# The order of an attention step on three engines, evictions one tick later, and three PSUM banks for the scores

## The chip, the cores and the metric

The kernel runs on one core of a Trainium2 chip. A core has a matrix engine (PE), a vector engine (DVE), an activation engine (ACT), a general engine (POOL) and a queue engine (SP), each with an instruction queue of its own that is worked off strictly in order. PE writes to eight PSUM banks, and DVE and ACT read them; everything else lies in SBUF. The metric is the device time of one launch in microseconds (us), the median over several runs.

## The reference

One layer of an encoder with two kinds of attention heads, run on a prompt of 1024 tokens and a sample of 512 tokens with the same weights; d_model is 1024, a head is 64 wide.

```python
hn = rms_norm(x, g_attn)
qa, ka, va, qd, kd, vd = split(hn @ w_in, 6)
oa = neighbourhood_attention(qa, ka, va, rpb)   # 8 heads, 8 x 16 window on a grid 64 wide
od = dilated_attention(qd, kd, vd, slopes)      # 8 heads, (window, dilation) = (128,1),(512,4),(2048,16)
x = x + concat(rms_norm(oa, g_na), rms_norm(od, g_dil)) @ w_out
x = x + (silu(rms_norm(x) @ w_gate) * (rms_norm(x) @ w_up)) @ w_down
y = rms_norm(x, g_final)
```

Each attention block is a softmax: `s = q k^T + bias`, `p = exp(s - max)`, `o = p v / sum(p)`. The whole is in float32.

## The kernel before

**Pairs and blocks.** The heads go in pairs: 16 pairs, first eight of the prompt, then eight of the sample, dilated ("b") and neighbourhood ("a") in turn: prompt b 0, prompt a 0, prompt b 1 and so on. A pair of the prompt has 16 blocks of 128 queries, eight of its first head and then eight of its second; a pair of the sample has 4 and 4. A block has 768 keys (prompt b), 384 (prompt a), 512 (sample b) or 256 (sample a).

**A block's work.** `scores` (L682) makes the negated scores on PE: two matmuls (high and low part of k, L698 and L699) into a PSUM bank `sc`, and for prompt b two more of 256 keys into a half of the bank `s2`. `softmax` (L732) adds the bias table and takes the minimum on DVE (L741; twice for prompt b), then has ACT make the exponentials (L748). `turn` (L750) transposes the block on PE in groups of up to four (L758, into the two banks `tp`, both of them for prompt b), has ACT write the fp16 high part (L762) and DVE the low part, which is the transposed value minus the high part (L763). `values` (L765) multiplies two blocks at a time by v on PE (L778) into half of the bank `pv`, and `head_out` (L781) sums it on DVE (L787).

**A step.** `step(g)` (L938) issues for block g the minimum and the exponentials, then `turn` for block g-1, the sum that is owed, every second step `values` for two older blocks, and `scores` for block g+1.

**Projections.** While a pair's blocks run, the next pair's q, k and v are projected: 24 matmuls of 512 columns (`mm3`, L155) for each accumulator, in the order v, q, k, for the prompt in two chunks. A *tick* is six of these matmuls. `target` (L923) says how many ticks have to be done by block j, and since j counts the blocks of a head and begins anew with the second head, the ticks of a pair come in its first half. In its second half, and until the end of its last block, no projection runs; then ticks follow in a row until k of the next pair is complete (`whole`). `after(n, fn)` (L160) puts `fn` off by n ticks. When an accumulator's fourth tick has been issued, `q_put`, `k_put` or `v_put` evicts it on ACT in the same tick (L396), and the low parts of q and k follow on DVE a tick later (L539, L507). A projection's weights are split by ACT (L124) and POOL (L125) before.

**What sets the order.** PE, DVE and ACT run the instructions as the program issues them (`manual_schedule`), except while the pairs 4, 7, 15 or the output projection are being projected (`loose`): there, in the blocks of prompt a 1, prompt b 3, sample b 3 and sample a 3, the tile scheduler orders them by its own estimates. POOL and SP are always ordered by the scheduler. After attention come the output projection, SwiGLU (by a seven-product scheme) and the down projection, which take the span from about 930 us to its end.

## Time and profile before

| | |
|---|---|
| time, median of 3 runs (lowest to highest) | 2112.17 us (2107.84 to 2113.09) |
| the profiled execution's own time | 2102.23 us |
| its span, first to last instruction | 2100.5 us |
| granted PE clock, mean over the span | 0.955 |
| PE busy | 1889.2 us, 90% |
| DVE, ACT, POOL busy | 64%, 44%, 40% |
| PE busy from 75.8 to 926.1 us (the attention) | 718.7 of 850.3 us, clock 0.93 |
| PE busy from 1050 us to the end | 1003.4 of 1050.5 us, clock 0.97 |

The granted clock is the share of full speed at which PE ran: 1.00 is 2.4 GHz and 0.50 is 1.2 GHz, and a mean between them says how much of a stretch was spent at either. PE's busy time is a union of overlapping matmuls, so it is not PE at its peak. Idle time of an engine that nobody waits for costs nothing; what counts is which wait ends last at each place.

### The profile page before, as it was taken

What the parts mean: (1) busy time and instruction counts of PE and PEld (TensorE: products, weight loads), DVE (VectorE), ACT (ScalarE), POOL (GpSimd) and SP (SyncE); (2) the same over time, 40 slices, a digit from 0 to 9 for tenths busy, and PEclk for the clock granted to TensorE, in tenths of its full rate; (3) what the DMA queues carried; (4) which work ended last, traced back from release to release, by engine and by line L of the source; (5) the groups of instructions that cost most, each with busy time, mean ns of one, the idle gap of its engine ahead of it and who ended that gap; (6) DMA issues with size and microseconds to landing.
All of it is one profiled execution on the core that took longest, in us unless ns stands there. A gap on an engine that the chain in (4) does not pass through costs nothing.

```text
span 2100.5 us, 28931 instructions
## 1 busy us (share of the span) xinstructions
PE 1889.2 (90%) x10450; PEld 1642.7 (78%) x10450; DVE 1334.3 (64%) x2626; ACT 913.9 (44%) x1731; POOL 845.1 (40%) x691
## 2 busy tenths in 40 slices
PE   5878879888977878899989999988999997999998
PEld 4667767766766666677879999988999996787886
DVE  6554455545664454566777777787767774766775
ACT  4444456544554454654443334344334332433441
POOL 3223224223223444411036676666666651652110
PEclk9998999999999989899999999999999999999999
DMA  9323124212243333535433434333344347876552
GB/s 270 89 65 82 37 69 120 73 55 75 68 95 75 92 96 85 166 102 173 157 110 119 136 122 126 101 117 114 116 121 123 109 121 251 296 235 218 201 184 100
DMA packets 218944, 265.98 MB, mean 127 GB/s; under 512 B 59584, under 2 KB 163152, under 8 KB 218800
## 3 DMA queue, kind: packets, MB, share of 16 engines
q1 hardware_dynamic: 196176, 179.57, 28.3%
q0 software_dynamic: 22624, 84.56, 13.6%
q8 instruction: 82, 1.34, 0.3%
q14 instruction: 62, 0.51, 0.1%
HBM read 202.71 MB, written 51.41 MB: 121 GB/s over the span
## 4 chain that ended last, share of the span: by engine, by line
PE 49%; DVE 7%; DMA 6%; issue 5%; ACT 4%; POOL 4%; SPq 0%; DVEq 0%; ACTq 0%; POOLq 0%
PE acc L155 19%; PE yacc L155 12%; PE zacc L155 8%; PE mmacc L155 7%; DMA wq<-in_w_down_dram 2%; POOL wlo L125 1%; POOL wq L1270 1%; DVE flo L1112 1%; DVE t L741 1%; ACT t L748 1%; ACT pT L762 1%; DMA left<-hid_d 1%; PE pt L210 1%; DMA hid_d<-as 1%; ACT ka L504 1%
## 5 line engine op out<-in xcount | busy, mean ns | idle before, releaser
L155 PE MATMUL acc<-dhi,left 128*128 128x512 f32 x924 | 291.7, 396 | 17.4 <-ACT left L1286 15.0
L763 DVE SCALAR_TENSOR_TENSOR pT<-pt,pT 128x512 f16<-128x512 f32 (+2 forms) x256 | 137.1, 555 | 240.3 <-ACT pT L762 240.0
L155 PE MATMUL acc<-hth,whi 128*128 128x512 f32 x576 | 237.9, 413 | 6.1 <-ACT hth L290 5.4
L155 PE MATMUL acc<-htl,whi 128*128 128x512 f32 x576 | 234.3, 407 | 6.2 <-POOL htl L293 3.4
L748 ACT ACTIVATE t<-t,mt 128x768 f32<-128x768 f32 (+3 forms) x192 | 138.4, 721 | 232.3 <-DVE mt L741 231.3
L155 PE MATMUL acc<-hth,wlo 128*128 128x512 f32 x576 | 234.8, 408 | 3.0 <-POOL wlo L125 2.7
L125 POOL TENSOR_TENSOR wlo<-wraw,whi 128x1024 fp32r<-128x1024 f32 x48 | 114.6, 2391 | 276.6 <-ACT whi L124 276.5
L155 PEld LDWEIGHTS acc<-dhi,left 128*128 128x128 f32 x924 | 175.3, 190 | 58.5 <-ACT left L1286 15.8
L1112 DVE TENSOR_TENSOR flo<-fs,fhi 128x512 fp32r<-128x512 f32 x176 | 173.8, 990 | 73.7 <-ACT fhi L1111 68.6
L758 PE MATMUL pt<-ident,t 128*128 128x128 f32 x768 | 132.0, 296 | 73.5 <-DVE pT L763 37.7
L1111 ACT ACTIVATE fhi<-fs 128x512 fp32r<-128x512 f32 x176 | 109.6, 629 | 180.3 <-POOL fs L1116 59.6
L155 PE MATMUL acc<-dlo,left 128*128 128x512 f32 x462 | 182.6, 395 | 0.3 <-DVE dlo L1260 0.3
L758 PEld LDWEIGHTS pt<-ident,t 128*128 128x128 f32 x768 | 95.4, 151 | 108.9 <-ACT t L748 48.2
L1116 POOL TENSOR_TENSOR fs<-fraw 128x512 f32<-128x512 f32 x88 | 133.4, 1531 | 79.6 <-DMA fraw<-in_w_up_dram 68.3
L1112 DVE TENSOR_TENSOR flo<-fraw,fhi 128x512 fp32r<-128x512 f32 x132 | 159.3, 1207 | 0.6 <-ACT fhi L1111 0.6
L1270 POOL TENSOR_TENSOR wq<-wq 128x512 f32<-128x512 f32 x55 | 90.4, 1655 | 163.6 <-DMA wq<-in_w_down_dram 160.6
L155 PEld LDWEIGHTS acc<-hth,wlo 128*128 128x128 f32 x576 | 112.3, 195 | 34.1 <-POOL wlo L125 8.9
L1111 ACT ACTIVATE fhi<-fraw 128x512 fp32r<-128x512 f32 x132 | 83.0, 629 | 128.0 <-PE yacc L155 96.8
L155 PEld LDWEIGHTS acc<-htl,whi 128*128 128x128 f32 x576 | 112.8, 196 | 29.8 <-DVE htl L293 4.4
L155 PEld LDWEIGHTS acc<-hth,whi 128*128 128x128 f32 x576 | 113.1, 196 | 29.3 <-ACT hth L290 6.1
L793 POOL TENSOR_TENSOR ob<-ob,den 128x256 f32<-128x256 f32 x48 | 30.6, 638 | 250.0 <-issue 128.3
L1287 DVE TENSOR_TENSOR left<-left,left 128x1408 fp32r<-128x1408 f32 x42 | 75.1, 1790 | 86.1 <-ACT left L1286 86.1
(223 smaller groups left out, 5009.6 us busy)
## 6 DMA issues: line engine op xcount, KB each, us to landing
wq<-in_w_down_dram SPq DMA_DIRECT2D x132, 256.0 KB
hid_d<-as POOLq DMA_DIRECT2D x22, 1344.0 KB, 8.2
left<-hid_d SPq DMA_DIRECT2D x42, 704.0 KB
wraw<-in_w_in_dram POOLq DMA_DIRECT2D x46, 512.0 KB, 4.7
fraw<-in_w_gate_dram SPq DMA_DIRECT2D x45, 512.0 KB
fraw<-in_w_up_dram SPq DMA_DIRECT2D x45, 512.0 KB
tabb<-in_tabb_dram POOLq DMA_DIRECT2D x8, 800.0 KB, 5.8
xh<-x_d SPq DMA_DIRECT2D x12, 512.0 KB
```

The source lines that it names most:

```text
L125: eng.tensor_tensor(out=lo, in0=src, in1=hi.bitcast(F32), op=ALU.subtract))
L155: latest[0] = nc.tensor.matmul(out=out, lhsT=a, rhs=b, start=first and i == 0, stop=i == last, skip_group_check=not first)
L210: nc.tensor.transpose(out=pts[k // 4][:, k % 4 * P:(k % 4 + 1) * P], in_=src[:, k * P:(k + 1) * P], identity=ident)
L748: nc.scalar.activation(t, t, AF.Exp, bias=mt, scale=-1.0, accum_out=k.den)
L758: nc.tensor.transpose(out=pt[:, c * P:(c + 1) * P], in_=k.t[:, (c0 + c) * P:(c0 + c + 1) * P], identity=ident)
L763: nc.vector.scalar_tensor_tensor(out=lo, in0=pt, scalar=16384.0, in1=hi, op0=ALU.mult, op1=ALU.subtract)
L793: nc.gpsimd.tensor_tensor(out=ob, in0=ob, in1=z, op=ALU.mult)
L1111: nc.scalar.activation(hi, src, AF.Copy)
L1112: nc.vector.tensor_tensor(out=lo, in0=src, in1=hi.bitcast(F32), op=ALU.subtract)
L1116: nc.gpsimd.tensor_tensor(out=o, in0=a, in1=b, op=op)
L1270: nc.gpsimd.tensor_tensor(out=src, in0=src, in1=other, op=q[1])
L1287: nc.vector.tensor_tensor(out=lo, in0=raw_lo, in1=hi.bitcast(F32), op=ALU.subtract)
```

## The change

Four edits in the attention steps. First, `step` issues the transposes of block g-1 first, and then, between the minimum of block g and its exponentials, the high part of block g-1; the low part comes after the exponentials and after the owed sum. The operations are the same and as many as before. Second, the eviction of an accumulator is put off (`after(2, ...)`, which within a tick means the next tick), and the low part still comes a tick after it, so both stand a tick later than before; K's four evictions take the halves in another order, and the first pair, which the opening projects, keeps its places. Third, the second part of prompt b's scores takes a whole bank from the same three `sc` banks as the first part, instead of half of the bank `s2`. Fourth, `values` takes the bank `pv` anew each time instead of its two halves in turn.

```diff
-BANKS = dict(mm=("mm", 2), sc=("sc", 2), s2=("s2", 1), pv=("pv", 1), tp=("tp", 2))
+BANKS = dict(mm=("mm", 2), sc=("sc", 3), pv=("pv", 1), tp=("tp", 2))
...
                 if i == 3:
-                    (q_put, k_put, v_put)[which](ch, acc)
+                    if pi:
+                        after(2, lambda: (q_put, k_put, v_put)[which](ch, acc))
+                    else:
+                        (q_put, k_put, v_put)[which](ch, acc)
                 yield
...
-            for i in range(2):
-                for o in (own[i], own[1 - i]):
-                    nc.scalar.activation(dst(ka[i], ch)[o], rev(acc[own[i]]), AF.Copy)
+            for n in range(2):
+                for i in range(2):
+                    nc.scalar.activation(dst(ka[i], ch)[own[i - n]], rev(acc[own[i]]), AF.Copy)
...
-            after(2, lows)
+            after(1 if pi else 2, lows)
...
-            after(2, low)
+            after(1 if pi else 2, low)
...
-                if "s2" not in heads:
-                    heads["s2"] = bank("s2", "s2")
-                sc = heads["s2"][:, k.j % 2 * 256:k.j % 2 * 256 + 256]
+                sc = bank("sc", "sc2")
...
-        nc.scalar.activation(t, t, AF.Exp, bias=mt, scale=-1.0, accum_out=k.den)
+        k.mt = mt
+
+    def exponentials(k):
+        nc.scalar.activation(k.t, k.t, AF.Exp, bias=k.mt, scale=-1.0, accum_out=k.den)
...
-            pt = pt.rearrange("p (c q) -> p c q", q=P)
-            hi, lo = (k.pT[:, n + c0:n + c0 + w] for n in (0, m))
+            k.turned.append((pt.rearrange("p (c q) -> p c q", q=P), *(k.pT[:, n + c0:n + c0 + w] for n in (0, m))))
+
+    def high(k):
+        for pt, hi, lo in k.turned:
             nc.scalar.activation(hi, pt, AF.Copy, scale=16384.0)
+
+    def low(k):
+        for pt, hi, lo in k.turned:
             nc.vector.scalar_tensor_tensor(out=lo, in0=pt, scalar=16384.0, in1=hi, op0=ALU.mult, op1=ALU.subtract)
...
-        n = heads["turn"] = 1 - heads.get("turn", 1)
-        if "pv" not in heads:
-            heads["pv"] = bank("pv", "pv")
-        pv = heads["pv"][:, n * 2 * P:(n + 1) * 2 * P].rearrange("p (b i d) -> p b i d", b=2, i=2)
+        pv = bank("pv", "pv", 2 * P).rearrange("p (b i d) -> p b i d", b=2, i=2)
...
     def step(g):
-        k = todo[g]
+        k, last = todo[g], pipe[-1] if pipe else None
+        if last:
+            turn(last)
         softmax(k)
-        if pipe:
-            turn(pipe[-1])
-        pipe.append(k)
+        if last:
+            high(last)
+        exponentials(k)
         while owed:
             head_out(owed.pop())
+        if last:
+            low(last)
+        pipe.append(k)
```

On ACT, in the second half of prompt b 0, before. `t_962` is a block, `pT_969` the transposed parts of the block in front of it; each block has one exponential (L748) and two high parts (L762).

```order
L748 ACTIVATE t_962,den_967<-t_962,mt_965 128x768
L762 ACTIVATE pT_969<-pt_970 128x512
L762 ACTIVATE pT_969<-pt_977 128x256
L748 ACTIVATE t_989,den_967<-t_989,mt_992 128x768
L762 ACTIVATE pT_995<-pt_996 128x512
L762 ACTIVATE pT_995<-pt_1003 128x256
```

And now; `t_977` is a block and `pT_968` belongs to the block in front of it.

```order
L769 ACTIVATE pT_968<-pt_969 128x512
L769 ACTIVATE pT_968<-pt_974 128x256
L752 ACTIVATE t_977,den_982<-t_977,mt_980 128x768
L769 ACTIVATE pT_996<-pt_997 128x512
L769 ACTIVATE pT_996<-pt_1002 128x256
L752 ACTIVATE t_1005,den_982<-t_1005,mt_1008 128x768
```

The exponentials have moved behind the two high parts of the block in front. On DVE, at the same place, before: two minima (L741, each with the row that reads out the accumulator), two low parts (L763) and the owed sum (L787).

```order
L741 ISA t_962,mt_963<-sc_947,tabb_838 128x512
L741 ISA mt_963 128x1
L741 ISA t_962,mt_965<-s2_557,tabb_838,mt_963 128x256
L741 ISA mt_965 128x1
L763 SCALAR_TENSOR_TENSOR pT_969<-pt_970,pT_969 128x512
L763 SCALAR_TENSOR_TENSOR pT_969<-pt_977,pT_969 128x256
L787 TENSOR_REDUCE ob_982<-pv_700 128x128
```

And now:

```order
L742 ISA t_977,mt_978<-sc_956,tabb_840 128x512
L742 ISA mt_978 128x1
L742 ISA t_977,mt_980<-sc2_959,tabb_840,mt_978 128x256
L742 ISA mt_980 128x1
L794 TENSOR_REDUCE ob_986<-pv_931 128x128
L773 SCALAR_TENSOR_TENSOR pT_968<-pt_969,pT_968 128x512
L773 SCALAR_TENSOR_TENSOR pT_968<-pt_974,pT_968 128x256
```

The sum has moved from behind the low parts to a place in front of them, and the second minimum reads a bank of its own (`sc2`) in place of `s2`. On PE the order in these steps is the same as before. At the end of prompt b 0, where ticks run in a row, ACT had, from the exponentials of the pair's last block on (qa and ka are the evictions of q and k, whi the split of weights, undo a scale for v):

```order
L748 ACTIVATE t_1223,den_1119<-t_1223,mt_1226 128x768
L762 ACTIVATE pT_1229<-pt_1230 128x512
L762 ACTIVATE pT_1229<-pt_1237 128x256
L535 ACTIVATE qa0_846<-acc_883 64x512
L535 ACTIVATE qa1_847<-acc_883 64x512
L489 ACTIVATE undo_1287<-up_1285 128x128
L504 ACTIVATE ka0_1309<-acc_1274 64x512 x2
L504 ACTIVATE ka1_1310<-acc_1274 64x512 x2
L124 ACTIVATE whi_1330<-wraw_902 128x1024
L504 ACTIVATE ka0_1309<-acc_1315 64x512 x2
L504 ACTIVATE ka1_1310<-acc_1315 64x512 x2
```

And now:

```order
L769 ACTIVATE pT_1239<-pt_1240 128x512
L769 ACTIVATE pT_1239<-pt_1245 128x256
L752 ACTIVATE t_1248,den_1140<-t_1248,mt_1251 128x768
L470 ACTIVATE va0_1296<-vT_607,vsc_783 128x512 x2
L538 ACTIVATE qa0_890<-acc_883 64x512
L538 ACTIVATE qa1_891<-acc_883 64x512
L492 ACTIVATE undo_1322<-up_1320 128x128
L507 ACTIVATE ka0_1337<-acc_1289 64x512
L507 ACTIVATE ka1_1338<-acc_1289 64x512
L507 ACTIVATE ka0_1337<-acc_1289 64x512
L507 ACTIVATE ka1_1338<-acc_1289 64x512
L124 ACTIVATE whi_1349<-wraw_904 128x1024
```

The second half of v's high part (`va`) has moved in here; before, it stood ahead of the blocks of the second head. K's evictions now take the two halves in turn (`ka0`, `ka1`, `ka0`, `ka1`), where two of one came first.

## Rows read from the trace of the kernel before

**Rows 1.** The page's first part: busy time of each engine over the whole program, share of the span and instructions.
```profile
PE 1889.2 (90%) x10450; PEld 1642.7 (78%) x10450; DVE 1334.3 (64%) x2626; ACT 913.9 (44%) x1731; POOL 845.1 (40%) x691
```

**Rows 2.** The view of waits between 60 and 950 us, where all the attention work lies: who sat idle for whom, us in total, times, the longest.
```profile
...
DVE pT L763 <- ACT pT L762: 240.0, 152, 9.1
...
PE pt L758 <- DVE pT L763: 37.7, 32, 2.5
...
PE pt L758 <- ACT t L748: 34.0, 32, 3.1
...
PE pv L778 <- DVE ob L787: 19.0, 31, 1.2
...
PE s L698 <- DVE mt L741: 13.9, 22, 1.8
...
PE sc L699 <- DVE kl L507: 12.8, 10, 1.7
```

**Rows 3.** The view in order of time, one step (one block) of the pair (prompt, b, 1) in the half without projections; columns: start, us, engine, line, operation, tiles, form, count, and in brackets the idle time before it and what ended it.
```profile
274.30 1.02 DVE L763 SCALAR_TENSOR_TENSOR pT<-pt,pT 128x512 f16<-128x512 f32 x2 [1.66 <-ACT pT L762]
...
275.05 0.88 PE L758 MATMUL pt<-ident,t 128*128 128x128 f32 x6 [1.85 <-DVE pT L763]
...
275.24 0.42 DVE L787 TENSOR_REDUCE ob<-pv 128x128 f32<-128x256 f32 x1
...
275.57 0.68 DVE L741 CUSTOM_DVE_ANT_0 t<-sc,tabb 128x512 f32<-128x512 f32 x1
...
276.40 0.48 DVE L741 CUSTOM_DVE_ANT_1 t<-s,tabb,mt 128x256 f32<-128x256 f32 x1
...
276.99 0.94 ACT L748 ACTIVATE t<-t,mt 128x768 f32<-128x768 f32 x1 [2.45 <-DVE mt L741]
...
277.93 0.85 ACT L762 ACTIVATE pT<-pt 128x512 f16<-128x512 f32 x2
...
278.53 1.02 DVE L763 SCALAR_TENSOR_TENSOR pT<-pt,pT 128x512 f16<-128x512 f32 x2 [1.64 <-ACT pT L762]
...
279.28 0.44 PE L758 MATMUL pt<-ident,t 128*128 128x128 f32 x2 [1.58 <-DVE pT L763]
...
279.47 0.68 DVE L741 CUSTOM_DVE_ANT_0 t<-sc,tabb 128x512 f32<-128x512 f32 x1
```

**Rows 4.** The view by stretches, over the twelve stretches of attention in which no projection matmul runs and the order of three engines is the program's own: three of prompt b, three of prompt a, three of sample b, three of sample a. Columns: stretch, us, busy us (and instructions) of PE, PEld, DVE, ACT, POOL, then the granted clock, DMA share and GB/s.
```profile
115.50:147.10 31.60, 20.97 (x173) 17.19 (x173) 18.07 (x54) 14.41 (x31) 4.87 (x8) 0.86 0.20 58
270.70:301.20 30.50, 18.57 (x172) 15.07 (x172) 17.82 (x53) 13.62 (x30) 4.36 (x8) 0.94 0.23 69
409.30:440.20 30.90, 20.56 (x173) 16.93 (x173) 17.95 (x53) 13.61 (x30) 4.38 (x8) 0.83 0.21 61
192.90:211.70 18.80, 13.72 (x86) 10.69 (x87) 9.68 (x30) 8.20 (x24) 6.60 (x10) 0.64 0.33 95
485.40:504.80 19.40, 11.68 (x86) 8.77 (x86) 10.93 (x33) 8.23 (x24) 6.57 (x10) 0.82 0.35 95
627.70:646.20 18.50, 11.66 (x90) 8.75 (x88) 9.55 (x30) 8.93 (x24) 3.96 (x7) 0.82 0.34 81
672.30:684.10 11.80, 6.54 (x55) 5.02 (x54) 7.39 (x17) 3.90 (x10) 1.30 (x3) 0.86 0.44 58
741.50:753.50 12.00, 6.49 (x55) 4.99 (x53) 7.38 (x17) 4.06 (x10) 0.86 (x2) 0.86 0.23 57
812.00:823.60 11.60, 6.73 (x55) 5.16 (x53) 7.20 (x17) 3.89 (x9) 0.86 (x2) 0.85 0.30 74
707.10:716.00 8.90, 4.58 (x32) 3.63 (x31) 5.25 (x17) 3.07 (x12) 1.15 (x2) 0.74 0.37 105
776.50:785.40 8.90, 4.86 (x31) 3.82 (x31) 5.25 (x17) 3.06 (x12) 0.69 (x2) 0.68 0.36 100
846.60:855.50 8.90, 4.57 (x31) 3.39 (x31) 5.25 (x17) 3.06 (x12) 0.69 (x2) 0.77 0.32 95
```

**Rows 5.** The view by line with shapes kept apart, 60 to 950 us: the exponentials of prompt a, sample b and sample a (busy us, mean ns of one | idle before).
```profile
L748 ACT ACTIVATE t<-t,mt 128x384 f32<-128x384 f32 x64 | 39.3, 614 | 62.0 <-DVE mt L741 61.1 <-DVE rqx L111 0.7 <-DVE den L790 0.2
...
L748 ACT ACTIVATE t<-t,mt 128x512 f32<-128x512 f32 x32 | 23.0, 720 | 40.3 <-DVE mt L741 40.3
...
L748 ACT ACTIVATE t<-t,mt 128x256 f32<-128x256 f32 x32 | 16.2, 507 | 28.2 <-DVE mt L741 28.2
```

**Rows 6.** The view in order of time around 240 us, a place where ACT stands ready and waits for the transposes.
```profile
239.55 0.82 PE L758 MATMUL pt<-ident,t 128*128 128x128 f32 x6
...
240.25 0.87 ACT L762 ACTIVATE pT<-pt 128x512 f16<-128x512 f32 x2 [0.38 <-PE pt L758]
```

**Rows 7.** The same view on PE, a step with projections: the second part of the scores.
```profile
253.35 0.39 PE L698 MATMUL s<-ka,qa 128*128 128x256 f32 x1 [1.29 <-DVE mt L741]
```

**Rows 8.** The same view on DVE: the two low parts of V's half (L472), at 686.9 us, when POOL is in a subtraction of 2.42 us, and at 668.7 us.
```profile
668.65 1.58 DVE L472 SCALAR_TENSOR_TENSOR va<-vT,vsc,va 128x256 f16<-128x256 f32 x2
...
686.87 3.03 DVE L472 SCALAR_TENSOR_TENSOR va<-vT,vsc,va 128x256 f16<-128x256 f32 x2 [0.66 <-ACT va L467]
```

**Rows 9.** The view by stretches over the three stages that the scheduler orders itself (blocks of prompt a 1, of prompt b 3, of sample b 3 and a 3); columns as in rows 4.
```profile
323.30:371.80 48.50, 45.65 (x292) 35.77 (x291) 31.46 (x99) 31.03 (x78) 19.17 (x25) 1.00 0.46 116
526.30:605.70 79.40, 69.69 (x470) 54.99 (x468) 52.36 (x132) 44.38 (x90) 17.87 (x23) 0.96 0.30 72
872.00:926.10 54.10, 46.53 (x270) 37.45 (x269) 40.57 (x129) 40.19 (x91) 9.65 (x16) 0.87 0.55 168
```

More of the change, by code (lines that the diff above doesn't have):

```diff
@@ L753, in turn @@
         k.pT = rb.tile([P, 2 * m, P], F16, tag="pT", name="pT", bufs=PTB)
+        k.turned = []
         for c0 in range(0, m, 4):
@@ L986, in hymba_layer_kernel @@
     turn(pipe[-1])
+    high(pipe[-1])
+    low(pipe[-1])
     while pipe:
```

## The prediction

> **What bounds the kernel now.** I read the page first. PE is busy 90% of the span, more than any other engine [rows 1], so only what shortens PE's work or its waits can count. The change touches the attention alone, so I next asked who waits there. DVE waits 240.0 us for the high parts on ACT [rows 2], which would cost nothing if PE did not wait behind it, but PE does: 37.7 us for low parts, 34.0 us for exponentials, 19.0 us for the sum over `pv`, 13.9 us for minima ahead of the second scores, and 12.8 us for the low part of k, together 117 us [rows 2].
>
> The view in order of time shows one step of that chain. DVE makes the minimum from 275.57 to about 276.89. ACT makes the exponentials from 276.99 and the high parts of the block in front from 277.93. Only then can DVE start the low parts, at 278.53, and PE's next transposes begin at 279.28, because they need the bank that the first low part frees. The transposes before them began at 275.05, so the step took 4.23 us, and PE idled 1.58 us of it [rows 3]. A step without the sum takes some 0.3 us less. So minimum, exponentials, high part and low part run one behind another, though the last two belong to another block than the first two.
>
> Where no projections run, nothing fills that idle time. The twelve such stretches in the program's own order take 31.6 + 30.5 + 30.9 = 93.0 us (prompt b), 18.8 + 19.4 + 18.5 = 56.7 (prompt a), 11.8 + 12.0 + 11.6 = 35.4 (sample b) and 3 x 8.9 = 26.7 (sample a), 211.8 us in all, and PE is busy in about 131 of them [rows 4]. That is where the change should pay.
>
> **The high part ahead, the low part beside the exponentials.** No instruction is added, and PE's order in a step stays. After the change a step is held by one of two loops. On ACT: transposes begin, the high parts begin 0.70 us later (240.25 less 239.55 [rows 6]), take about 0.80 until the engine is free (their pair spans 0.85 with its end overlapped), the exponentials 0.94 [rows 3], and a hand-over of 0.1 (276.99 less 276.89) lets the next transposes start: 2.54 us. On DVE: the minimum 1.32 us (275.57 to 276.89), the low parts 0.94 (278.53 to 279.47) and half of the 0.33 that a sum takes (275.24 to 275.57) [rows 3]: 2.43 us and hand-overs. Since both loops have nearly one length and wait for each other, I take 2.7 us in place of about 4.1. A stretch has eight transposes, seven steps and an end with transposes and values of about 2 us: 7 x 2.7 + 2 = 21 us instead of 31, and three of them give 93 - 63 = 30 us.
>
> For the other kinds the same loop through ACT gives, with exponentials of 0.61, 0.72 and 0.51 us [rows 5] and one high part instead of two: prompt a 0.6 + 0.4 + 0.61 + 0.1 = 1.7, say 1.8; sample b 0.7 + 0.5 + 0.72 + 0.1 = 2.0, say 2.1; sample a 0.5 + 0.35 + 0.51 + 0.1 = 1.45, say 1.5. (The starts and high parts here are estimates, the 0.70 and 0.80 of prompt b scaled to fewer keys.) With an end of 1.2, 1.5 and 1.1 us the stretches become 7 x 1.8 + 1.2 = 13.8, 3 x 2.1 + 1.5 = 7.8 and 3 x 1.5 + 1.1 = 5.6 us. Gains: 56.7 - 41.4 = 15, 35.4 - 23.4 = 12 and 26.7 - 16.8 = 10 us. First sum: 67 us. Bounds: at the bare loops (2.54, 1.7, 2.0, 1.45) it is 74; if the step loses only a part of DVE's wait for ACT, with 3.4 us for prompt b (25.8 us a stretch, 16 gained) and half of the gain for the rest, it is 34.
>
> **Scores in three banks.** PE waits at the second part of the scores until both minima of the block before are done (1.29 us at 253.35 [rows 7]), since the two halves of `s2` share a bank. In the new order the bank it takes was last read by the first minimum, a half step earlier. Of 13.9 us [rows 2] I take 8 as gained: the rest lies in the stretches counted above. Bounds 0 and 13.9. The sum over `pv` comes earlier on DVE, and its 19.0 us lie mostly in the stretches, where they are counted. Nothing queues for the bank that `s2` gives up.
>
> **Evictions a tick on.** An accumulator's bank comes back a tick later, but is wanted again only four ticks later, so I cost that at nothing; if the slack were gone, PE would wait for a bank at each accumulator. `whole` also comes a tick later, so one more tick of matmuls runs ahead of the next pair's first scores, and it covers the 12.8 us that PE waits there for k's low part [rows 2]: 8 us gained. Against it stands v: in a sample a pair both halves of v's split now fall among the ticks at the pair's end. SP's transposes of the first half must land before ACT may begin the second, and k's evictions queue behind that on ACT. Three places at 1.3 us: 4 us lost, so 4 us remain. Bounds -8 and +13.
>
> Rows 8 weigh a rule here. The two low parts of v took 1.58 us at 668.65 and 3.03 us at 686.87, beside a subtraction on POOL [rows 8]. The Trainium skill (SBUF — State Buffer, "Who interferes with whom") says that a DVE instruction with two inputs in SBUF and a GpSimd instruction that reads SBUF exclude each other. The trace agrees, and by that rule three more pairs of low parts could meet the subtraction, 3 x 1.5 = 4.5 us more lost.
>
> **The clock.** In the stretches PE ran at 1.2 GHz for twice the missing clock times their length: 23 us in prompt b, 27 in prompt a, 10 and 14 in the sample, 74 us of 211.8 [rows 4]. Today much of that is hidden in waiting. PE's full-speed work per step, estimated from busy time less half of these spells (18.57 less 1.8 over eight steps for the stretch at 270.70), is 2.1 us for prompt b and in the same way 1.0, 1.2 and 0.65; at 1.2 GHz it is 4.2, 2.05, 2.4 and 1.3, more than the new step for the first three. If the spells stay as long, they cost (1 - 2.7/4.2) x 23 = 8, 12% of 27 = 3 and 12% of 10 = 1 us. I subtract 10.
>
> **The sum.** 67 + 8 + 4 - 10 = 69 us. The stages that the scheduler orders I leave at zero, with 10 us to either side. Against the profiled execution: 2102.2 - 69 = 2033 us. The median of the runs shown is 10 us above that execution, so the forecast is 2112 - 69 = 2043 us. Its own range is a gain of 45 to 95 us, 2017 to 2067.
>
> **Rivals.** *The clock takes it back.* If PE runs the whole of every new stretch at 1.2 GHz, prompt b has steps of 4.2 us and gains nothing (30 lost), prompt a has 2.05 (7 x 2.05 + 1.2 = 15.6, 5 lost), sample b 2.4 (3 lost). The 10 us of the clock term are then in this already: 67 - 38 + 8 + 4 = 41 us gained, 2071 us. For it: clocks of 0.64 to 0.86 in eleven of the twelve stretches; against it: 0.94 in one that is no fuller than the others [rows 4], and shorter waits now. The Trainium skill (TensorE: Matmul & The Clock Gate, "A second HAM failure mode: psum-queue depth-cycling") tells of a kernel that goes through PSUM banks in turn and pauses PE briefly each time, until its clock swings between the levels; by it this rival's 2071 us is what to expect. No row here separates that from the longer waits of today.
>
> *Slower: the scheduler's own stages.* The three stages that the scheduler orders anew take 48.5 + 79.4 + 54.1 = 182 us with PE busy for 45.65 + 69.69 + 46.53 = 162 of them [rows 9]. There high parts stand ahead of exponentials too, and if the scheduler's estimates place a transpose late, ACT holds the exponentials behind it. At the PE share of the worst fixed stretches, about 0.6, these stages would take 162/0.6 = 270 us, 88 lost: 2112 - 69 + 88 = 2131 us. It decides once PE's share there falls below 162/(182 + 69) = 0.65. Against it: it is 0.94, 0.88 and 0.86 now, and ready projections fill PE.
>
> *Nothing.* If the transposes turned out to be held by something else (the banks `tp`, which stay two), the step would stay at 4.1 us: 2112 us. Against it: in the new order the low part that frees the bank follows the high part at once.
>
> *More.* If the waits of rows 2 go whole and the clock rises with PE's share, the gain passes 95 us, to about 2005.
>
> **How the numbers follow.** The forecast has 0.62, the clock rival 0.15, more 0.08, the slower rival 0.06, nothing 0.05, and a small gain of 6 to 25 us 0.04. A measurement of this kernel can tell about 0.3%, 6 us, from no change. Faster is 0.62 + 0.15 + 0.08 + 0.04 = 0.89, the same 0.05, slower 0.06. The range 2005 to 2088 takes in the forecast, the clock rival and most of "more".
>
> **What would show it.** Right: DVE's wait for the high parts falls from 240 us to under 60; in a step of prompt b without projections transposes follow each other at 2.5 to 2.9 us; the stretch at 270 us takes about 21; PE's waits in the attention fall from 117 to under 60 us; the pair's first scores wait under 1 us for k. Wrong: steps above 3.5 us; a granted clock under 0.7 in all stretches; PE's share in the three scheduled stages under 0.8; a new wait of PE for an accumulator's bank or for transposed v.

## The result and the profile after

The changed kernel takes 1995.28 us (median of 4 runs, 1991.46 to 2001.32) where the kernel before takes 2110.01 (2106.89 to 2113.09): a ratio of 0.946 with an interval of 0.943 to 0.949, so 114 us gained. The forecast was 69 us, 2043, and the whole range, rivals included, ended at 2005; the kernel came out 10 us below it. The profiled execution took 1991.46 us, 110.8 less than the one profiled before.

The page's first part shows PE 45 us less busy with the same 10450 instructions, and a larger share of the span [rows 1]:

```profile
PE 1843.8 (93%) x10450; PEld 1619.5 (81%) x10450; DVE 1320.6 (66%) x2626; ACT 915.6 (46%) x1731; POOL 843.3 (42%) x691
```

The same work takes less PE time, and the mean granted clock is 0.973 where it was 0.955, so part of the gain is the clock's. The view of waits between 60 and 950 us, where L763 are the transposes, L752 the exponentials, L769 and L773 the high and low parts, and L701/L702 the scores:

```profile
DVE pT L773 <- ACT pT L769: 130.9, 116, 8.5
...
PE pt L763 <- ACT t L752: 39.7, 53, 1.2
...
PE pt L763 <- DVE pT L773: 4.3, 7, 1.3
...
PE sc L702 <- DVE kl L510: 3.6, 7, 1.6
...
PE sc L701 <- DVE mt L742: 1.8, 3, 1.2
```

PE's waits for low parts (37.7 us before), for the second scores (13.9) and for k (12.8) are small now, and none for the sum is left among the longest [rows 2]. What is left is a wait for exponentials, which is the loop through ACT. DVE still waits 130.9 us for high parts, but PE no longer waits behind that. Two steps of prompt b 1 without projections, in order of time:

```profile
248.40 0.69 DVE L742 CUSTOM_DVE_ANT_0 t<-sc,tabb 128x512 f32<-128x512 f32 x1
...
248.55 0.87 PE L763 MATMUL pt<-ident,t 128*128 128x128 f32 x6
...
249.30 0.87 ACT L769 ACTIVATE pT<-pt 128x512 f16<-128x512 f32 x2 [0.80 <-PE pt L763]
...
250.06 0.94 ACT L752 ACTIVATE t<-t,mt 128x768 f32<-128x768 f32 x1
250.08 0.99 DVE L773 SCALAR_TENSOR_TENSOR pT<-pt,pT 128x512 f16<-128x512 f32 x2
...
250.99 0.68 DVE L742 CUSTOM_DVE_ANT_0 t<-sc,tabb 128x512 f32<-128x512 f32 x1
...
251.14 0.87 PE L763 MATMUL pt<-ident,t 128*128 128x128 f32 x6 [1.02 <-ACT t L752]
...
253.73 0.88 PE L763 MATMUL pt<-ident,t 128*128 128x128 f32 x6
```

High parts start 0.75 us after the transposes, exponentials 0.76 later, the next transposes 1.08 after that: a step of 2.59 us, where it was 4.23 [rows 3]. Low parts and exponentials begin together, at 250.06 and 250.08. DVE is nearly full beside it: from minimum to minimum it also takes 2.59 us, and it is busy for 16.96 of the stretch's 19.60 us. The stretches without projections, columns as in rows 4 (prompt b, then prompt a, then one of sample b and one of sample a):

```profile
112.80:132.40 19.60, 15.54 (x172) 13.62 (x170) 16.99 (x51) 13.41 (x31) 4.46 (x8) 1.00 0.24 76
243.60:263.20 19.60, 15.55 (x172) 13.62 (x171) 16.96 (x51) 13.45 (x31) 3.78 (x7) 1.00 0.28 89
365.90:385.50 19.60, 15.52 (x172) 13.62 (x171) 16.93 (x51) 13.45 (x31) 5.07 (x8) 1.00 0.24 76
176.10:192.20 16.10, 11.60 (x87) 9.01 (x85) 8.62 (x27) 8.36 (x23) 5.61 (x8) 0.74 0.44 114
429.10:442.70 13.60, 8.65 (x86) 6.34 (x85) 9.18 (x30) 7.82 (x21) 4.94 (x7) 1.00 0.49 132
563.40:576.50 13.10, 8.64 (x85) 6.34 (x84) 8.67 (x27) 8.14 (x23) 4.34 (x7) 1.00 0.60 117
601.00:608.20 7.20, 4.99 (x55) 3.67 (x53) 4.31 (x11) 4.29 (x10) 1.60 (x3) 1.00 0.48 96
...
629.50:634.30 4.80, 2.85 (x31) 2.21 (x30) 2.71 (x11) 2.77 (x10) 1.52 (x3) 1.00 0.73 161
...
sum 137.60, PE 99.01 PEld 80.19 DVE 98.43 ACT 85.58 POOL 36.84; mean PE 8.25 PEld 6.68 DVE 8.20 ACT 7.13 POOL 3.07
```

They take 137.6 us instead of 211.8, and eleven of twelve run at a clock of 1.00. In the sample, DVE also has less to do in them: 11 instructions instead of 17 [rows 4], and two of the six are q's low part. The three stages that the scheduler orders, against 182 us and clocks of 1.00, 0.96 and 0.87 before [rows 9]:

```profile
285.10:334.10 49.00, 47.22 (x304) 37.92 (x303) 31.70 (x99) 31.39 (x77) 18.95 (x24) 1.00 0.41 110
464.10:544.80 80.70, 70.03 (x468) 55.22 (x466) 51.48 (x130) 45.61 (x92) 21.29 (x25) 0.96 0.28 74
773.60:823.90 50.30, 45.61 (x296) 37.01 (x295) 39.20 (x124) 38.84 (x86) 6.29 (x10) 1.00 0.49 153
```

So the stretches explain 74 of the 110.8 us. Most of the rest lies in the halves *with* projections, for which the forecast had 12 us (8 for the banks, 4 for the evictions). Here is the first half of prompt b 1 before:

```profile
231.00:270.70 39.70, 36.90 (x240) 30.08 (x240) 20.76 (x57) 19.57 (x40) 11.02 (x11) 0.93 0.14 32
```

And after, with PE busy throughout and at full clock:

```profile
212.30:243.60 31.30, 31.30 (x234) 26.79 (x233) 22.14 (x61) 19.02 (x38) 11.72 (x12) 1.00 0.19 43
```

### The profile page after: what moved, and what is told of

It reads as the page before. It is cut to its first block, busy times and chain, and to the rows that moved or that the text cites. A ratio compares the mean times of both kernels' runs of the same rounds, so it can differ in the third digit from the quotient of the medians.

```text
span 1989.6 us, 28959 instructions
## 1 busy us (share of the span) xinstructions
PE 1843.8 (93%) x10450; PEld 1619.5 (81%) x10450; DVE 1320.6 (66%) x2626; ACT 915.6 (46%) x1731; POOL 843.3 (42%) x691
## 4 chain that ended last, share of the span: by engine, by line
PE 47%; DMA 5%; DVE 4%; issue 3%; POOL 2%; ACT 1%; SPq 0%; DVEq 0%; POOLq 0%; ACTq 0%
PE acc L155 16%; PE yacc L155 13%; PE zacc L155 8%; PE mmacc L155 8%; DMA wq<-in_w_down_dram 2%; DMA left<-hid_d 1%; POOL wq L1284 1%; DVE flo L1126 1%; PE pt L210 1%; DMA hid_d<-as 1%; DMA wo_raw<-in_w_out_dram 0%; DVE left L1301 0%; ACT left L1300 0%; DVE dlo L1274 0%; POOL as L1244 0%
## 5 line engine op out<-in xcount | busy, mean ns | idle before, releaser
L773 DVE SCALAR_TENSOR_TENSOR pT<-pt,pT 128x512 f16<-128x512 f32 (+2 forms) x256 | 136.8, 553 | 132.5 <-ACT pT L769 130.9
L125 POOL TENSOR_TENSOR wlo<-wraw,whi 128x1024 fp32r<-128x1024 f32 x48 | 114.5, 2388 | 197.5 <-ACT whi L124 197.5
L769 ACT ACTIVATE pT<-pt 128x512 f16<-128x512 f32 (+2 forms) x256 | 118.9, 489 | 162.6 <-PE pt L763 159.3
L763 PE MATMUL pt<-ident,t 128*128 128x128 f32 x768 | 122.8, 282 | 44.2 <-ACT t L752 39.7
L763 PEld LDWEIGHTS pt<-ident,t 128*128 128x128 f32 x768 | 89.8, 143 | 76.6 <-ACT t L752 56.9
L752 ACT ACTIVATE t<-t,mt 128x768 f32<-128x768 f32 (+3 forms) x192 | 137.9, 718 | 25.8 <-DVE mt L742 23.3
```

The costliest lines, as they stand in the source:

```text
L125: eng.tensor_tensor(out=lo, in0=src, in1=hi.bitcast(F32), op=ALU.subtract))
L752: nc.scalar.activation(k.t, k.t, AF.Exp, bias=k.mt, scale=-1.0, accum_out=k.den)
L763: nc.tensor.transpose(out=pt[:, c * P:(c + 1) * P], in_=k.t[:, (c0 + c) * P:(c0 + c + 1) * P], identity=ident)
L769: nc.scalar.activation(hi, pt, AF.Copy, scale=16384.0)
L773: nc.vector.scalar_tensor_tensor(out=lo, in0=pt, scalar=16384.0, in1=hi, op0=ALU.mult, op1=ALU.subtract)
```

## The experiments

The theory to test (A): the step's order pays more than forecast because the clock stays up and because it also pays in the halves with projections, and the late evictions pay more than 4 us. The rival (B): the step gave the forecast 57 us (67 less 10 for the clock), and something in the other edits the rest. Each kernel was run beside the kernel before on the same chip. The last column is (1 - ratio) x 2110, with the interval's bounds worked out in the same way.

| kernel | median us | ratio (interval) | us gained |
|---|---|---|---|
| the change | 1995.3 | 0.946 (0.943 to 0.949) | 114 (108 to 120) |
| step alone | 2027.9 | 0.960 (0.959 to 0.962) | 84 (80 to 87) |
| banks alone | 2100.5 | 0.995 (0.993 to 0.997) | 11 (7 to 14) |
| late evictions alone | 2082.0 | 0.986 (0.983 to 0.988) | 31 (26 to 35) |
| the change, old evictions | 2009.0 | 0.952 (0.949 to 0.955) | 101 (95 to 107) |
| the change, old banks | 2004.2 | 0.950 (0.947 to 0.954) | 105 (97 to 112) |
| only q late | 2100.3 | 0.996 (0.994 to 0.997) | 9 (6 to 12) |
| only k late | 2108.7 | 1.000 (0.998 to 1.002) | 0 (-3 to 4) |
| only v late | 2125.9 | 1.007 (1.005 to 1.010) | -15 (-20 to -10) |
| q and k late | 2108.9 | 0.999 (0.997 to 1.001) | 3 (-1 to 6) |
| the change, q early again | 2035.3 | 0.965 (0.963 to 0.967) | 74 (69 to 78) |
| the change, k early again | 2003.1 | 0.952 (0.949 to 0.954) | 102 (96 to 108) |
| the change, v early again | 2001.6 | 0.949 (0.948 to 0.951) | 107 (103 to 111) |
| the change, low parts twice | 2053.3 | 0.973 (0.970 to 0.975) | 57 (52 to 63) |
| the change, ticks spread | 1944.9 | 0.922 (0.920 to 0.924) | 165 (160 to 169) |
| spread, old evictions | 1951.8 | 0.926 (0.924 to 0.928) | 156 (152 to 160) |
| before, ticks spread | 2028.2 | 0.961 (0.958 to 0.964) | 82 (76 to 88) |

Profiled executions can be laid side by side by the starts of each pair's first exponentials: the eight prompt pairs, the five sample pairs from b 0 to b 2, and all that follows.

| us | start | prompt pairs | five sample pairs | the rest |
|---|---|---|---|---|
| before | 75.8 | 580.9 | 175.7 | 1268.1 |
| step alone | 79.2 | 523.1 | 157.7 | 1266.6 |
| late evictions alone | 76.2 | 578.6 | 160.7 | 1267.2 |
| only v late | 80.1 | 603.0 | 179.8 | 1266.8 |
| the change, old evictions | 75.0 | 509.7 | 158.0 | 1260.6 |
| the change | 77.4 | 509.9 | 141.9 | 1260.5 |
| the change, q early again | 77.4 | 532.4 | 156.9 | 1261.8 |
| the change, v early again | 75.0 | 508.4 | 148.4 | 1264.8 |
| the change, k early again | 76.9 | 514.1 | 151.1 | 1258.8 |
| the change, ticks spread | 75.6 | 482.2 | 132.2 | 1253.8 |
| spread, old evictions | 75.3 | 482.7 | 130.0 | 1261.8 |

### One edit at a time, and the change without one

The kernel before with `step`, `turn`, `high`, `low` and `exponentials` as in the change, all else old:

```diff
+        if last:
+            high(last)
+        exponentials(k)
         while owed:
             head_out(owed.pop())
+        if last:
+            low(last)
```

> The kernel before with the order of the step alone (high part ahead of the exponentials, low part behind them and behind the owed sum); old banks, old evictions. Theory A, the step pays more than forecast because PE's clock stays up in the stretches once its waits are shorter: 75 to 85 us gained, about 2030 us, stretches of prompt b at 20 us or less and a granted clock of 0.95 or more in most of the twelve. Theory B, the step gave the 57 us of the forecast and the other edits gave the rest: about 2053 us. If the step depends on the third score bank, its transposes in prompt b stay over 3.2 us apart here and under 30 us are gained.

It gained 84 us: theory A's figure. (The profiled executions differ by 73.9 us only, since the one of the kernel before ran some 10 us below its median; those 10 us have no place in the table.) Its stretches, of prompt b twice, of prompt a twice (a 0 and a 3) and of sample a:

```profile
116.90:136.50 19.60, 16.07 (x172) 13.38 (x171) 16.42 (x49) 13.44 (x31) 4.23 (x7) 1.00 0.34 84
249.40:269.00 19.60, 16.07 (x171) 13.38 (x170) 16.38 (x49) 13.38 (x31) 4.15 (x7) 1.00 0.39 98
...
181.40:194.50 13.10, 8.64 (x86) 6.34 (x85) 8.39 (x26) 7.78 (x22) 5.64 (x8) 1.00 0.41 124
...
575.60:591.90 16.30, 12.52 (x89) 9.98 (x88) 8.88 (x27) 9.17 (x25) 4.40 (x7) 0.69 0.43 92
...
711.50:717.90 6.40, 3.36 (x30) 2.66 (x31) 4.58 (x16) 3.01 (x10) 1.33 (x2) 0.89 0.53 153
```

Prompt b is at 19.6 us without the third bank, so the step does not depend on it. All twelve take 147.6 us, 64 less than before. The clock is 1.00 in seven of the twelve stretches, a bare majority: two of prompt a and the three of sample a stand between 0.69 and 0.89. Prompt a 0 took 13.1 us at 1.00 and a 3 took 16.3 at 0.69 (13.1 at 1.00 in the change), which prices a low clock at about 3 us a stretch. The prompt pairs together gained 57.8 us, of which their six stretches make up 45.6 (149.7 [rows 4] less 104.1); 12 us lie outside the stretches, the most of it in prompt b's halves with projections. That of prompt b 1 fell from 39.7 to 35.6 us.

The score banks and `pv` alone, then the change without them:

```diff
-BANKS = dict(mm=("mm", 2), sc=("sc", 2), s2=("s2", 1), pv=("pv", 1), tp=("tp", 2))
+BANKS = dict(mm=("mm", 2), sc=("sc", 3), pv=("pv", 1), tp=("tp", 2))
...
+                sc = bank("sc", "sc2")
```

> The kernel before with three score banks and pv taken anew, old step and old evictions. Forecast term: 8 us, bounds 0 and 13.9, so 2096 to 2110 us. Theory A (the banks matter little by themselves): 2102 us or more, PE's wait for the minimum ahead of the second scores gone in the first halves of prompt b. Rival (the banks are what unlocks prompt b): 2090 us or less, prompt b stretches shorter by over 4 us each.

> The changed kernel with the two old score banks, the bank s2 and the two halves of pv put back. Banks alone gained 10 to 12 us; on top of the step the kernel without the late evictions stood 19 us lower than with the step alone. If the banks add up: 8 to 12 us given back, 2003 to 2007 us. If they are worth more behind the new step (the first halves of prompt b are then held by the half banks): 15 to 19 us, 2010 to 2014 us. In both, the first halves of prompt b are longer by 1 to 3 us each and the stretches without projections stay at 19.6 us.

Alone they gained 11 us; taken from the change they gave back 9 (2004.2 against 1995.3). The first half of prompt b 1 got 2.4 us longer and the stretches of prompt b stayed at 19.6. The banks add up, as the forecast had it, though the 9 us are near the noise: the intervals of the 114 and the 105 us overlap.

The late evictions alone (the second edit of the change, with k's order of halves), and the change with the old ones:

> The kernel before with the evictions one tick later alone. Forecast term: 4 us net, bounds -8 and +13, so 2106 us. Theory A: the tick that moves from a pair's first half into the end of the pair in front costs nothing there and saves about 2 us in each of 13 pairs, so about 26 us gained, 2084 us, PE's wait for k's low part near nothing. Theory B: 2102 to 2110 us.

> The changed kernel with its evictions and their low parts put back to where they were before. Theory A: 20 to 26 us given back, 2015 to 2021 us, 12 us of waits of PE for k's low part back. Theory B: 4 us given back, 1999 us.

31 us alone and 14 within the change (2009.0 against 1995.3), where the forecast had 4; the 14 lie between the two theories. By the table above, those 14 us are in the five sample pairs (158.0 against 141.9) and not in the prompt. Alone, the sample pairs gain nearly as much (175.7 against 160.7) and the prompt 2.3 us; the profiled executions differ by 17.7 us, and where the rest of the 31 lies is not shown.

### Which of the three evictions

In the kernel before, one or two accumulators late:

```diff
-                    (q_put, k_put, v_put)[which](ch, acc)
+                    if pi and which == 0:
+                        after(2, lambda: (q_put, k_put, v_put)[which](ch, acc))
+                    else:
+                        (q_put, k_put, v_put)[which](ch, acc)
```

(0 is q, 1 is k, 2 is v; `which < 2` is q and k. The low parts of the late ones go with them.)

> The kernel before with q's eviction and low part alone a tick later. In the kernel before, q's low part (1.39 us on DVE) stands at the head of each stretch without projections of the sample pairs, because its tick is the last before the stretch; a tick later it falls behind the stretch. Theory Q (this is what the eviction edit mostly gave): the six sample stretches get 2 to 3 us shorter, 12 to 16 us gained, about 2098 us. Theory K (the gain is the tick that the next pair's k waits for): under 5 us gained here, stretches as before.

> The kernel before with k's eviction, its order of halves and its low part alone a tick later. Theory Q: PE's 12.8 us of waits for k's low part go, 8 to 12 us gained, about 2103 us, the sample stretches as before. Theory K: over 15 us gained, 2097 us or less. If the moved tick is no cover at all: no gain.

> The kernel before with v's eviction alone a tick later (all that follows it, the scale, the two halves' parts and the transposes, comes a tick later too). The three evictions together gained 31 us, q alone 9 and k alone nothing. If the terms add up, v gives the rest: 15 to 22 us, about 2092 us. If the gain comes only from q and k together (the stretch that loses q's low part and the boundary that loses its wait for k), v alone gives nothing or loses the 4 us of the forecast: 2105 to 2114 us.

> The kernel before with the evictions of q and k a tick later, v's as before. If v gives the rest: 9 to 10 us gained, 2100 us. If q and k help each other: 25 to 31 us gained, about 2082 us.

q gave 9, k 0, v cost 15 and q with k gave 3, so neither sum nor pair makes 31; both readings that were on record for the last two fell. K gained nothing although PE's waits for its low part fell from 12.8 to 4.0 us there. The same question was then put to the changed kernel, one accumulator early again:

```diff
-                    if pi:
+                    if pi and which != 0:
```

> The changed kernel with q's eviction and low part alone put back to their earlier tick. All three put back cost 14 us, and by the trace these lie in the six sample pairs from sample b 0 to sample a 2 (141.9 us became 158.0). If q's low part at the head of the stretches (1.39 us on DVE, six times, and what the lower clock adds behind it) is the cause: 8 to 14 us given back, 2003 to 2009 us, sample a stretches at 6.0 us or more instead of 4.75. If the tick ahead of k is the cause: under 3 us, the stretches as in the changed kernel.

> The changed kernel with k's eviction, its order of halves and its low part alone put back. If q is the cause: PE waits for k's low part again at each pair (about 1.4 us, some 10 us in all), 3 to 10 us given back, 1998 to 2005 us, the stretches at 7.2 and 4.75 us as in the changed kernel. If the tick ahead of k is the cause of the 14 us: 12 to 14 us, 2007 to 2009 us.

> The changed kernel with v's eviction alone put back. In the kernel before, v alone a tick later cost 16 us. If that holds here too, this is 4 to 16 us faster than the changed kernel, 1979 to 1991 us. If v's later parts are needed because they, too, leave the sample stretches (q and k alone gave 1 us in the kernel before, all three 31): 5 to 14 us slower, 2000 to 2009 us.

(The 141.9 and 158.0 us named there are those of five pairs, to sample b 2.) Put back alone, q costs 40 us, far above the 8 to 14 expected and more than all three together. K costs 8. V costs 6 by the medians, but its interval (103 to 111 us gained) overlaps that of the change (108 to 120), so this is not clear of noise. By the table, q's 40 us lie in two places: 15.0 in the five sample pairs, where all three put back cost 16.1, and 22.5 in the prompt, where all three put back cost nothing.

The part in the sample can be read on DVE, in sample a 0 of the kernel with q early again:

```profile
654.72 0.42 DVE L773 SCALAR_TENSOR_TENSOR pT<-pt,pT 128x256 f16<-128x256 f32 x1 [2.84 <-ACT pT L769]
655.18 1.39 DVE L542 SCALAR_TENSOR_TENSOR qa<-acc,qa 64x512 fp32r<-64x512 f32 x2
656.60 0.42 DVE L742 CUSTOM_DVE_ANT_0 t<-sc,taba 128x256 f32<-128x256 f32 x1
```

q's low part (L542) stands between two steps at the very head of the stretch, where nothing covers it. The high part that DVE waits for ahead of it is late on ACT, behind q's eviction (L538) and a part of v (L444) that has moved into the same tick:

```profile
652.34 1.20 ACT L538 ACTIVATE qa<-acc 64x512 fp32r<-64x512 f32 x2 [2.23 <-PE acc L155]
653.56 0.72 ACT L444 ACTIVATE v<-vT,vsc 128x512 f16<-128x512 f32 x1
654.31 0.38 ACT L769 ACTIVATE pT<-pt 128x256 f16<-128x256 f32 x1
```

The stretches of sample b and sample a, 7.2 and 4.8 us in the change, are then

```profile
623.50:633.20 9.70, 6.61 (x54) 4.84 (x54) 7.24 (x17) 4.84 (x12) 1.56 (x3) 0.82 0.29 69
...
654.60:662.10 7.50, 4.02 (x31) 3.23 (x31) 5.19 (x17) 3.67 (x14) 1.92 (x4) 0.78 0.42 106
```

with the 17 instructions on DVE of the kernel before, and with a lower clock. The six stretches of the sample take 51.4 us instead of 36.0. So the tick just before a stretch is the dear one: what is put off into it runs in the stretch's head. With all three put back the six take 43.5 us, so there only about half of the 16 us lies in the stretches. Another 6 are PE's waits for k's low part in these five pairs (7.4 us against 1.7 in the change), and the rest is not placed.

The part in the prompt is a meeting of q's work with v's. With v late and q early, both come just ahead of the last tick before the stretch of prompt b. In prompt b 1 of the kernel with q early:

```profile
247.09 1.39 DVE L542 SCALAR_TENSOR_TENSOR qa<-acc,qa 64x512 fp32r<-64x512 f32 x2
248.49 3.30 DVE L475 SCALAR_TENSOR_TENSOR va<-vT,vsc,va 128x512 f16<-128x512 f32 x2
...
252.58 0.58 PE L701 MATMUL sc<-ka,qa 128*128 128x256 f32 x1 [2.92 <-DVE mt L742]
```

The next minimum stands behind both, and PE waits 2.92 us for it. V's low parts (L475) run beside a subtraction on POOL (L125, from 248.22 for 2.35 us) and take 3.30 us; in the change they take 1.41 at the same place (237.54), POOL's subtraction begins only behind them (240.01), and PE does not wait. Prompt b 0 and b 2 show the 3.3 us too. The three pairs of prompt b are 4.7, 5.2 and 3.7 us longer than in the change; the rest of the 22.5 us is not traced to a cause. The same meeting is in the kernel before with v alone late (q's low part at 114.05, v's at 115.45, PE waits 3.25 us at 119.20), and there the prompt takes 22.1 us more. So v's eviction must not move without q's, and this is one reason why the single runs do not add up. With k early, PE waits for k's low part again, in the view of waits between 60 and 950 us:

```profile
PE sc L702 <- DVE kl L510: 13.2, 9, 1.6
```

With v early the five sample pairs take 6.5 us more, though the stretches keep their length, and there a rule met in the prediction returns with the other sign. In that kernel v's low parts (L475) stand beside POOL's subtraction (L125) again:

```profile
606.31 2.39 POOL L125 TENSOR_TENSOR wlo<-wraw,whi 128x1024 fp32r<-128x1024 f32 x1 [0.87 <-ACT whi L124]
...
606.74 2.64 DVE L475 SCALAR_TENSOR_TENSOR va<-vT,vsc,va 128x256 f16<-128x256 f32 x2
```

Over all sixteen of these instructions in the sample (the view of one line: shortest, median and longest in ns) that kernel shows

```profile
L475 DVE SCALAR_TENSOR_TENSOR va<-vT,vsc,va x16: 470/950/2247, 592.5 to 770.9; 128x256 f16<-128x256 f32 x16
```

and the change

```profile
L475 DVE SCALAR_TENSOR_TENSOR va<-vT,vsc,va x16: 470/478/868, 609.0 to 769.2; 128x256 f16<-128x256 f32 x16
```

The prediction, by the Trainium skill (SBUF — State Buffer, "Who interferes with whom"), feared that more of them would meet POOL's subtraction. The trace agrees that they exclude each other: the first of the two low parts at 606.74 takes 2.25 us, where one takes 0.47 by itself, and ends 0.3 us behind the subtraction. But the later tick took them mostly out of POOL's way (median 478 ns instead of 950). That this is what the 6.5 us are made of is not shown.

### The clock

The change with each low part issued twice, so that DVE's loop is longer again:

```diff
         for pt, hi, lo in k.turned:
-            nc.vector.scalar_tensor_tensor(out=lo, in0=pt, scalar=16384.0, in1=hi, op0=ALU.mult, op1=ALU.subtract)
+            for _ in range(2):
+                nc.vector.scalar_tensor_tensor(out=lo, in0=pt, scalar=16384.0, in1=hi, op0=ALU.mult, op1=ALU.subtract)
```

> The changed kernel with each low part issued twice on DVE (the same values are written again). The step of prompt b without projections gets one more pair of low parts, 0.99 us: 2.59 + 0.99 = 3.6 us, stretches 7 x 3.6 + 2 = 27 us instead of 19.6, and some 4 us each for prompt a, 2 for the sample; in all 45 to 50 us slower, about 2043 us. On the clock: if PE's waits of about 1.5 us in each step are what lets the clock fall, the granted clock in the stretches of prompt b goes from 1.00 to 0.95 or less; if it needs something else (what stood in the old order), it stays at 1.00 and PE waits in full speed.

58 us slower than the change, more than expected. The stretches of prompt b came to the 27 us worked out:

```profile
112.80:140.10 27.30, 18.37 (x174) 15.22 (x173) 25.58 (x69) 14.21 (x31) 4.11 (x6) 0.94 0.19 59
253.30:280.40 27.10, 17.26 (x173) 13.73 (x173) 25.41 (x69) 14.41 (x31) 4.92 (x8) 1.00 0.18 59
391.20:419.20 28.00, 19.57 (x173) 16.53 (x173) 25.70 (x70) 14.18 (x31) 4.80 (x8) 0.88 0.18 57
```

The clock fell in two of three, to a mean of 0.94, where it was 1.00 in the change and 0.88 before. Longer waits in the steps (up to 1.86 us here, in the change 1.02) do bring lower clocks, but not in each stretch: the middle one has the same waits and stays at 1.00. What decides between two such stretches stays open. The other profiles agree: of the 21 stretches of prompt b in the seven kernels with the old step and the ticks in the first half, all run below 1.00 (0.79 to 0.94), and of the 21 in the seven with the new step and single low parts 20 run at 1.00.

### Ticks over both heads

`target` counts the blocks of a head. With the pair's blocks counted instead, projections run in both halves, and the stretches are gone:

```diff
-        while spent[0] < target(k.pi, k.j):
+        while spent[0] < target(k.pi, k.i * counts[k.pi] // 2 + k.j):
```

> The changed kernel with the projections' ticks spread over both heads of a pair (their target counts the pair's blocks, not the head's). If the stretches without projections are all that is left to gain: PE's idle 4.1 us in each prompt b, 4.5 to 5 in prompt a, 2.2 and 2.0 in the sample go, 30 to 38 us gained, about 1960 us. If evictions and low parts that now fall among the second head's steps hold up DVE's chain there: 0 to 10 us gained or a loss, 1985 to 2005 us.

> The kernel before, old step, banks and evictions, with the projections' ticks spread over both heads of a pair. If the old step only cost time because nothing filled the waits: most of the 115 us is had without the change, 1990 to 2010 us, and the change would be worth 45 to 65 us on top of it. If the waits of the old step stay in the path also with a tick in each step: 2040 to 2070 us, and the change is worth as much with spread ticks as without.

> The kernel with spread ticks (1944.9 us) with the evictions put back to where they were before. If late evictions pay because they keep DVE work out of the stretches without projections, there is nothing left to gain here, since no such stretch is left: within 5 us, 1940 to 1950 us. If they pay at the pairs' boundaries: 8 to 14 us slower, 1953 to 1959 us.

On the change it gained another 50 us, more than the 30 to 38 expected: at 1944.9 us this is the fastest of all. The five sample pairs, PE busy for 128.29 of 132.20 us:

```profile
557.80:690.00 132.20, 128.29 (x834) 105.96 (x834) 78.67 (x209) 87.68 (x190) 74.43 (x68) 1.00 0.49 116
```

The thirteen pairs of the table got 37 us shorter (27.7 and 9.7), about what PE idled in the twelve stretches (137.6 less 99.0); 7 more lie behind these pairs. On the old step the same edit gained 82 us, and the change is worth 83 on top of it (2028.2 less 1944.9). That lies between the two theories on record, above what "nothing filled the waits" allowed: also with a tick in each step the old order keeps PE waiting. With spread ticks and the old step, between 60 and 950 us:

```profile
PE s L698 <- DVE mt L741: 21.3, 24, 1.9
PE pv L778 <- DVE ob L787: 19.4, 26, 2.1
```

With the new step the largest of PE's waits there adds up to 7.5 us. The late evictions are worth 7 us here, between the two cases expected (within 5, or 8 to 14). By the table these are not in the thirteen pairs but behind them (1253.8 against 1261.8), which fits the reading that in the sample pairs late evictions pay by what they keep out of the stretches.

## Why the prediction was right and wrong

The mechanism of the step held. What failed are three terms of the sum: the step was given nothing in the halves with projections, where alone it gained some 12 us; the clock term kept the old slow spells, most of which went; and the evictions were put at 4 us, where within the change they are worth 14.

- **The step was right.** It forecast 2.7 us between transposes of prompt b and measured 2.59, by the loop through ACT that the prediction named (2.54). The first sum of 67 us for the stretches came out at 64 with the step alone, slow clocks in five of the twelve included, and at 74 in the change, where the late evictions also take work out of the sample's.
- **The clock was wrong.** "If the spells stay as long, they cost" 8, 3 and 1 us (12 in all, of which the sum subtracts 10): they did not stay. In the change the clock is 1.00 in eleven of twelve stretches; only prompt a 0 pays, some 3 us, behind a bias table that came late (last section). The rival that the clock takes it back, with the rule on banks taken in turn (the Trainium skill, TensorE: Matmul & The Clock Gate, "A second HAM failure mode: psum-queue depth-cycling"), did not happen: in the change PE takes three banks in turn, waits up to 1.02 us in a step and stays at full clock in prompt b. The spells of before went as the waits got shorter; the doubled low parts brought some of them back. For the stretches with the clock 57 us were forecast, where the step alone took out 64.
- **The halves with projections were left out.** The forecast let the step gain only where no projections run. The step alone gained some 12 us in the prompt outside the stretches, because there too PE waited (prompt b 1: 36.90 us busy of 39.70, at a clock of 0.93).
- **The banks were right:** 8 us forecast, 9 to 11 measured.
- **The evictions were mis-sized:** +8 for k and -4 for v forecast; within the change the three are worth 14, and v's loss did not show (v early alone is not faster; the 1.3 us a place behind the -4 stand in no row). PE's waits for k's low part fell from 12.8 to 3.6 us, as meant. What was missed is q: its low part, two of DVE's 17 instructions in the sample stretches of rows 4, leaves the head of the stretch. The forecast followed the put-off work to the pair's end only, and not to the end of the first half.
- **The sum.** 57 + 8 + 4 = 69. Measured from the step alone, the banks and the late evictions one after another: 84, then 17 more (101), then 13 more (114). The step is the larger miss, 27 us: by the profiles 7 in the stretches and some 12 in the prompt's halves with projections, the rest without a place. The last two are 9 over each, in that order.
- **What would show it.** Spacing, stretches and PE's waits (the five kinds that were 117 us are 39.7 + 4.3 + 1.8 + 3.6 = 49) came as said; DVE's wait for high parts did not fall under 60 us, and PE does not wait behind it any more; k's low part still cost up to 1.6 us. Scheduled stages kept PE's share (0.96, 0.87, 0.91), so the slower rival has nothing for it. "More" came nearest, with its 2005 us too high by 10: the clock rose with PE's share, but the waits of rows 2 fell to 49 us and did not go whole.

## What to carry to other kernels

A stage in which PE waits for over a third of the time at a low clock (131 of 211.8 us busy here) can be worth more than its waits: when the waits went, the clock mostly came back, and so a term for the clock should not simply take the old spells over. When work is put off by a fixed count of ticks, look at which tick is the last before a stretch without cover: on each engine, what lands in that tick stands at the head of the stretch, and moving one of several such pieces can put it onto another (q back alone cost 40 us, all three back 14, and 22.5 of the 40 came in the prompt, where q's work met v's). And before an order inside a step is tuned, see whether the filler is spread evenly: one line on the ticks gained 50 us on top of all of this.

## What the runs showed of the hardware

A single longer wait can stand just ahead of a fall of the clock. Prompt a 0 without projections took 16.1 us at 0.74 in the change and 13.1 us at 1.00 with the step alone. The one difference found between the two is a bias table that landed late in the change:

```profile
182.50 0.56 DVE L742 CUSTOM_DVE_ANT_0 t<-sc,taba 128x384 f32<-128x384 f32 x1 [1.35 <-DMA taba<-e_d]
```

PE's next transposes came after a wait of 1.25 us, at 183.93, where its waits had been 0.88 and 0.31, and from there the clock stood at 1.2 GHz for some 10 us (three transposes took 0.90 us instead of 0.55). That the wait is what made it fall is not shown: with the doubled low parts waits of 1.8 us left one stretch at 1.00.

And beside POOL's subtraction one and the same DVE instruction of 128x256 took up to 2247 ns, where the shortest took 470: nearly five times as long.
